# Selection rounds paced by a load table, fp32 products in two parts, and index products two heads behind, in a hybrid recurrence and sparse-attention block

## The chip, the cores and the metric

The kernel runs on one core of one Trainium2 chip. The metric is the device time of one execution in microseconds (us). Its engines are TensorE (PE, matrix products; PEld is its weight load), VectorE (DVE), ScalarE (ACT), GpSimd (POOL) and SyncE (SP), whose queue issues nearly all DMAs. Each engine works through its own instructions in order.

## The reference

One layer over 512 tokens of width 2048. The input is normalised and projected; branch A is a gated linear recurrence (8 heads), branch B attends to 128 keys for each query, which an indexer with 16 heads picks; gates merge the branches, an output projection goes into the residual, and a norm ends it. The parts that matter here:

```
k_idx = layernorm(k_idx_raw)                                  # keys' norm
rel_scores = relu(einsum('bthd,bsd->bths', qi_blk, k_idx))    # index products, 16 heads
score = einsum('bths,bth->bts', rel_scores, wi_blk)
score = where(visible, score, -inf)
top_val, top_idx = top_k(score, 128)                          # selection
bias = bias_table[t5_bucket(top_idx - t_pos)]                 # bias by distance
logits = where(valid, logits + bias, -inf)
# branch A, by chunks: cumulative decays, scores inside a chunk, a state between chunks
```

## The kernel before

**Products.** Every large product is done in high and low float32r parts: `split` (L71) makes the high part on ScalarE and the low part, source minus high part, on VectorE, and `mm3` (L75) does three products of them. Weights come through SP into `wr` (two buffers) and are split into `wh` and `wl` by `prep` (L157), two groups ahead of the products that read them; a load of `wr` is held until VectorE has made the `wl` from that buffer.

**What sets the order.** A hand-written order: a job runs its products on PE and calls `pump` (L189) after every 12 products of 512 columns or 24 of 256. `pump` gives each of six lanes one step, in the order hgrn, top, att, norm, misc, t5. What a lane issues in a step stands in the engines' queues ahead of what comes next. I call the stretch from one pump to the next a step.

**The recurrence** (`hgrn_gen`, L736) runs once for each of four pairs of heads, in the order 3, 2, 0, 1, which I call the first to the fourth recurrence. It has eight levels, a step each. In a level PE computes many small score products `hl` from `hq` and `hk` (L753); then VectorE scales `hq` by decays (L757 in level 0, L764 later) and makes the next decays `tot` (L769), POOL scales `hk` (L766), and a mask copy takes the scores (L780). The next level's `hl` needs `hq` and `hk` scaled. After the levels come state products, and at the end a norm over `hz`, on ScalarE Ln and Exp, then the output block on VectorE (four operations at L841 and L842) and the two parts `hy` of its result.

**The selection** (`top_gen`, L649) finds each query's 128 best keys on VectorE: for three blocks of queries (b = 1, 2, 3, with 256, 384 and 512 columns) 16 rounds each, a round being MAX8 (L663) and MATCH_REPLACE8 (L664), and then a flag pass over the block (L666). How many rounds a step gets is set by a credit: `R.hot` is true in the eight levels, and a step then adds 0.55 rounds; in all others it adds 1.75.

**The index** (`qidx_evac`, L619, and `idx_gen`, L629): a projection tile of a head (12 products of 384 columns) is split into `qih` and `qil`; the head's index products `sc`, nine in three blocks, are put in the lane when the next head's tile has been split, one head behind. ScalarE takes them with a relu and VectorE sums them into `M`.

**Keys' norm** (`kidx_gen`, L596) sums over partitions with a product of ones and plain fp32 data, once for the mean and once for the variance. **The bias** (`t5_gen`, L459) selects bias rows by an fp32 product with a one-hot table (L472), writes them to DRAM (`t5_d`), loads them back shifted by one element a partition (`bf`, two loads of 512 KB), and flips the partitions with an fp32 product (L487) for two heads at a time, four flips.

Of the kernel before, what the change touches and what calls it, by code (L numbers as in the profile page):

```python
# [26 lines left out]
F32 = mybir.dt.float32  # L27
FR = mybir.dt.float32r
AF = mybir.ActivationFunctionType
# [5 lines left out]
T, D = 512, 2048  # L35
NK = D // 128
H, HD = 8, 128
# [13 lines left out]
def hybrid_block(ctx, tc, x, norm_w, w_in, lb_table, gnorm_a, q_norm_w, kv_norm_w, w_uq,  # L51
# [3 lines left out]
    V, A, G, PE, SP = nc.vector, nc.scalar, nc.gpsimd, nc.tensor, nc.sync  # L55
# [38 lines left out]

    ya_d = dram.tile([2, H, 128, T], F32, name="ya_d")
    yb_d = dram.tile([2, H, 128, T], F32, name="yb_d")
    t5_d = dram.tile([H, 384], F32, name="t5_d")
    gate_d = dram.tile([48, 128, T], F32, name="gate_d")
    bh_d = dram.tile([H, 128, 256], F32, name="bh_d")
    m21_d = dram.tile([2, 128, 8, 256], F32, name="m21_d")  # L100
# [12 lines left out]
    def leave(name):  # L113
        pools.pop(name)[0].__exit__(None, None, None)

    R = SimpleNamespace(hot=False)


    specs = []
# [60 lines left out]
    lanes = {name: deque() for name in ("hgrn", "top", "att", "norm", "misc", "t5")}  # L180

    late = [[], []]
# [275 lines left out]

    def t5_gen():  # L459
        rb = R.i.tile([128, H], F32, name="rb")  # L460
        oh = R.i.tile([128, 384], F32, name="oh")
        tl = R.i.tile([H, 384], F32, name="tl")
        flip = R.i.tile([128, 128], F32, name="flip")
        far = R.i.tile([H, 1], F32, name="far")
        G.memset(rb, 0.0)
        SP.dma_start(rb[0:32], rel_bias)
        SP.dma_start(oh, c_buckets)
        SP.dma_start(flip, c_flip)
        yield
        yield  # L470
        ps = bank("t5")
        PE.matmul(ps[:H, :384], rb, oh, start=True, stop=True)  # L472
        V.tensor_copy(far, ps[:H, 0:1])
        V.tensor_scalar(tl, ps[:H, :384], far, None, op0=OP.subtract)
        late[1].append(lambda: SP.dma_start(t5_d, tl))
        yield
        yield
        yield
        for h in range(0, H, 2):
            if h % 4 == 0:  # L480
                bf = R.i.tile([128, 4, 256], F32, name="bf")
                SP.dma_start(bf, bass.AP(tensor=t5_d.tensor, offset=t5_d.offset + h * 384,
                                         ap=[[1, 128], [384, 4], [1, 256]]))
                yield
                yield
            ps = bank("t5")
            PE.matmul(ps, flip, bf[:, h % 4:h % 4 + 2, :], start=True, stop=True)  # L487
            e = R.i.tile([128, 2, 256], F32, name="nt", bufs=2)
            V.tensor_copy(e, ps.rearrange("p (h c) -> p h c", h=2))
            late[1].append(lambda h=h, e=e: SP.dma_start(bh_d[h:h + 2].rearrange("h p c -> p h c"), e))  # L490
            yield
# [102 lines left out]
            yield  # L594

    def kidx_gen():  # L596
        ps = bank("ns")
        mm(ps, ones, R.kx[:, 0, :], True, True)
        t = R.i.tile([128, T], F32, name="nt", bufs=2)
        V.scalar_tensor_tensor(t, ps, -1.0 / 128, R.kx[:, 0, :], op0=OP.mult, op1=OP.add)  # L600
        s = R.i.tile([128, T], F32, name="nsq", bufs=2)
        A.activation(s, t, AF.Square)
        yield
        yield
        ps = bank("ns")
        mm(ps, ones, s, True, True)
# [10 lines left out]
    waiting = []  # L617

    def qidx_evac(h0):  # L619
        def evac(c, ps):  # L620
            qh = R.q.tile([128, 384], FR, name="qih", bufs=2)
            ql = R.q.tile([128, 384], FR, name="qil", bufs=2)
            split(qh, ql, ps)
            if waiting:
                lanes["misc"].append(waiting.pop())
            waiting.append(idx_gen(h0 + c, qh, ql))
        return evac

# [20 lines left out]
    def top_gen():  # L649

        credit = 0.0
        V.memset(R.M[:, 0:128], 0.0)
        for b in range(4):
            V.memset(R.M[0:64, MO[b] + b * 128 + 64:MO[b] + b * 128 + 128], NEG)
        for b in (1, 2, 3):
            m = R.M[:, MO[b]:MO[b] + b * 128 + 128]
            for i in range(16):
                while credit < 1:
                    yield
                    credit += 0.55 if R.hot else 1.75  # L660
                credit -= 1
                m8 = R.s.tile([128, 8], F32, name="m8", bufs=2)
                V.max(m8, m)  # L663
                V.match_replace(m, m8, m, GONE)  # L664
                if i == 15:
                    V.tensor_scalar(m, m, -2e38, NEG, op0=OP.is_gt, op1=OP.mult)  # L666
# [69 lines left out]
    def hgrn_gen(p):  # L736
        f, k, q = (hg[p, n] for n in "fkq")
# [31 lines left out]
            V.tensor_tensor(nt, tv[:, :, 0], tv[:, :, 1], op=OP.mult)  # L769
            return nt  # L770

        R.hot = True
        for l in range(8):
            if l == 4:
                G.memset(S, 0.0)
            ps = bank("hl")
            scores(l, ps)
            tot = decay(l)
            if l < 6:
                V.copy_predicated(near, R.levels[:, l:l + 1, :].to_broadcast([128, 8, 32]),  # L780
                                  ps[:, 0:256].rearrange("p (n t) -> p n t", n=8))
# [10 lines left out]
        R.hot = False  # L792
        kd = R.h.tile([128, 2, 3, 128], F32, name="hkd")
        for c in range(2):
            pt = bank("hkt")
# [3 lines left out]
        yield  # L799
        while (p, "v") not in hg:  # L800
            yield
        v = hg[p, "v"]
        st = R.h.tile([128, 2, 3, 128], F32, name="hst")
        for c in range(2):
# [13 lines left out]
        for c in range(2):  # L818
            po = bank("ho")
            for j in range(4):  # L820
                sl = slice(j * 128, (j + 1) * 128)
                mm(po[:, sl], v[:, j, c * 128:(c + 1) * 128], S[:, 4 * c + j, :], j == 0, j == 0)
                if j:
                    mm(po[:, sl], st[:, c, j - 1, :], q[:, c, sl], False, True)
            A.activation(o[:, c], po, AF.Copy)
            A.activation(sq[:, c], po, AF.Square)
            yield
            zs.append((place(p, [128, T], FR, "hzh", ("hkd", "hst")[c]),
                       place(p, [128, T], FR, "hzl", ("hq", "hS")[c])))
            split(*zs[c], sq[:, c])  # L830
        yield
        for c in range(2):
            ps = bank("hz")
            mm(ps, ones_r, zs[c][0], True, False)
            mm(ps, ones_r, zs[c][1], False, True)
            A.activation(sq[:, c], ps, AF.Ln, bias=eps, scale=1.0 / 128)
        A.activation(sq, sq, AF.Exp, scale=-0.5)
        yield
        for c in range(2):
            r = sq[:, c]  # L840
            V.scalar_tensor_tensor(r, o[:, c], c_gw, r, op0=OP.mult, op1=OP.mult)  # L841
            V.tensor_tensor(r, r, gate[:, c], op=OP.mult)  # L842
        yield
        for c in range(2):
            y = [place(p, [128, T], FR, f"hy{i}", (("hkd", "hst"), ("hq", "hS"))[i][c]) for i in range(2)]
            split(*y, sq[:, c])
            for i in range(2):
                late[1].append(lambda y=y[i], i=i, h=2 * p + c: SP.dma_start(ya_d[i, h], y.bitcast(F32)))
# [308 lines left out]
                 qidx_evac(2 * p), width=384)  # L1157

    def end_index():
        lanes["misc"].append(waiting.pop())  # L1160
# [363 lines left out]
```

## Time and profile before

| what | us |
|---|---|
| runs of the kernel before (three) | 1381.38, 1379.5, 1381.48; median 1381.38 |
| the profiled execution's own time | 1379.72 |
| its span, first to last instruction | 1377.9 |
| PE busy | 1353.1 |
| VectorE busy | 1072.2 |
| ScalarE busy | 654.3 |
| POOL busy | 83.0 |

The profile is one execution. Times in its rows count from the span's start. In a timeline row the first number is the start, the second how long it took; a matmul's record is longer than the time by which it holds back the next one, because products overlap in the array, so what a product costs is read from end to end or from start to start. In brackets stands the engine's idle time before the row and what ended it. The granted clock is TensorE's, as a share of 2.4 GHz; it knows two levels, 2.4 and 1.2 GHz.

### The profile page before, as it was taken

The page shows a single profiled execution, that of the slowest core. Times are in us where ns is not written, and L with a number is a line of the kernel's source. Part 1 is how long each engine was busy: PE and PEld are TensorE (multiplying, and loading weights), DVE is VectorE, ACT ScalarE, POOL GpSimd, SP SyncE. Part 2 cuts the span into 40 slices and gives each one's busy share as a digit, 9 for nine tenths or more (in the row PEclk, how much of TensorE's full clock was granted, in tenths as well). Part 3 has the DMA queues.
Part 4 walks back from the last instruction along what each step waited for, and adds up shares of the span by engine and source line. Part 5 has one row for each costly group of instructions (what it writes and reads, how often), then busy time and mean ns, then how long its engine had stood idle before and what let it go on. Part 6 is the DMA issues. An engine that isn't in the chain of part 4 may idle for free. (4 is left out here: it accounts for less than half of the span.)

```text
span 1377.9 us, 26785 instructions
## 1 busy us (share of the span) xinstructions
PE 1353.1 (98%) x10940; PEld 1253.3 (91%) x10940; DVE 1072.2 (78%) x1738; ACT 654.3 (47%) x1047; POOL 83.0 (6%) x85
## 2 busy tenths in 40 slices
PE   8999999999999999999999989999999999999997
PEld 7888999999999999998989778878888888899996
DVE  7796889988898888877777889675556558899856
ACT  6545445545554444446734442635534333454435
POOL 2100000000000000000030303050101100000000
PEclk9999999999999999999999999999999999999999
DMA  6334345444444344445234323434755556643464
GB/s 205 93 107 138 108 138 169 153 138 143 134 153 136 114 135 138 153 138 188 65 104 121 120 56 120 134 114 141 274 191 192 188 179 218 211 146 121 157 211 168
DMA packets 143597, 203.73 MB, mean 148 GB/s; under 512 B 10433, under 2 KB 84850, under 8 KB 143346
## 3 DMA queue, kind: packets, MB, share of 16 engines
q1 hardware_dynamic: 143186, 201.69, 46.0%
q8 instruction: 86, 1.41, 0.4%
q10 hardware_dynamic: 288, 0.33, 0.1%
q14 instruction: 37, 0.30, 0.1%
HBM read 166.84 MB, written 35.14 MB: 147 GB/s over the span
## 5 line engine op out<-in xcount | busy, mean ns | idle before, releaser
L150 ACT ACTIVATE bh<-wr 128x768 fp32r<-128x768 f32 x128 | 108.1, 845 | 220.5 <-issue 119.6
L152 ACT ACTIVATE wh<-sv 128x512 fp32r<-128x512 f32 x256 | 151.7, 622 | 85.2 <-DVE sv L145 66.2
L73 DVE TENSOR_TENSOR wl<-wr,wh 128x1024 fp32r<-128x1024 f32 (+1 forms) x104 | 127.1, 1222 | 61.0 <-ACT wh L72 60.6
L78 PE MATMUL pp<-sh,wl 128*128 128x256 f32 x624 | 172.8, 277 | 0.0
L76 PE MATMUL pp<-sh,wh 128*128 128x256 f32 x624 | 172.8, 277 | 0.0
L77 PE MATMUL pp<-sl,wh 128*128 128x256 f32 x624 | 172.7, 277 | 0.0
L153 DVE TENSOR_TENSOR bl<-wr,bh 128x768 fp32r<-128x768 f32 x128 | 122.3, 956 | 54.4 <-ACT bh L150 54.0
L72 ACT ACTIVATE wh<-wr 128x1024 fp32r<-128x1024 f32 (+1 forms) x104 | 108.1, 1040 | 116.8 <-PE acc L77 59.7
L154 DVE TENSOR_TENSOR wl<-sv,wh 128x1024 fp32r<-128x1024 f32 x128 | 156.5, 1223 | 7.5 <-ACT wh L152 1.1
L76 PE MATMUL acc<-xh,wh 128*128 128x512 f32 x304 | 122.4, 403 | 0.0
L78 PE MATMUL acc<-xh,wl 128*128 128x512 f32 x304 | 118.7, 391 | 0.0
L77 PE MATMUL acc<-xl,wh 128*128 128x512 f32 x304 | 118.5, 390 | 0.0
L77 PEld LDWEIGHTS pp<-sl,wh 128*128 128x128 f32 x624 | 117.3, 188 | 0.0
L78 PEld LDWEIGHTS pp<-sh,wl 128*128 128x128 f32 x624 | 117.3, 188 | 0.0
L76 PEld LDWEIGHTS pp<-sh,wh 128*128 128x128 f32 x624 | 117.3, 188 | 0.0
L76 PE MATMUL pp<-xh,bh 128*128 128x256 f32 x416 | 114.9, 276 | 0.0
L77 PE MATMUL pp<-xl,bh 128*128 128x256 f32 x416 | 114.9, 276 | 0.0
L78 PE MATMUL pp<-xh,bl 128*128 128x256 f32 x416 | 114.9, 276 | 0.0
L76 PE MATMUL acc<-yh,wh 128*128 128x512 f32 x256 | 100.2, 392 | 0.0
L78 PE MATMUL acc<-yh,wl 128*128 128x512 f32 x256 | 99.8, 390 | 0.0
L77 PE MATMUL acc<-yl,wh 128*128 128x512 f32 x256 | 99.7, 390 | 0.0
L145 DVE TENSOR_TENSOR sv<-wr 128x512 f32<-128x512 f32 x128 | 87.9, 687 | 7.3 <-DMA wr<-in_w_in_dram 3.6
(384 smaller groups left out, 3693.4 us busy)
## 6 DMA issues: line engine op xcount, KB each, us to landing
wr<-in_w_in_dram SPq DMA_DIRECT2D x136, 512.0 KB, 3.6
wr<-in_w_out_dram SPq DMA_DIRECT2D x32, 512.0 KB, 3.7
mg<-gate_d SPq DMA_DIRECT2D x48, 256.0 KB, 3.9
gate_d<-c SPq DMA_DIRECT2D x44, 256.0 KB, 5.0
wr<-in_w_in_dram SPq DMA_DIRECT2D x36, 256.0 KB, 3.1
wr<-in_w_pa_dram SPq DMA_DIRECT2D x16, 512.0 KB, 4.7
wr<-in_w_pb_dram SPq DMA_DIRECT2D x16, 512.0 KB, 3.2
x<-in_x_dram SPq DMA_DIRECT2D x8, 512.0 KB, 6.5
```

The costliest lines, as they stand in the source:

```text
L72: A.activation(hi, src, AF.Copy)
L73: V.tensor_tensor(lo, src, hi.bitcast(F32), op=OP.subtract)
L76: PE.matmul(ps, lh, rh, start=first, stop=False, skip_group_check=True)
L77: PE.matmul(ps, lh, rl, start=False, stop=False, skip_group_check=True)
L78: PE.matmul(ps, ll, rh, start=False, stop=last, skip_group_check=True)
L145: V.tensor_tensor(sv[:, 0:2, :], b[:, 1:3, :], b[:, 0:1, :].to_broadcast([128, 2, 256]), op=OP.add)
L150: A.activation(bh, b[:, 1:4, :], AF.Copy)
L152: A.activation(vh[:, i:i + 2, :], sv[:, i:i + 2, :], AF.Copy)
L153: V.tensor_tensor(bl, b[:, 1:4, :], bh.bitcast(F32), op=OP.subtract)
L154: V.tensor_tensor(vl, sv, vh.bitcast(F32), op=OP.subtract)
```

## The change

Four edits.

1. **Rounds by room.** `R.hot` becomes `R.load`, a number in us that the recurrence sets for every step (eight values for the levels, others for the steps behind them). `top_gen` adds 2.7 less the load to its credit each step, and a round takes 0.4 + 0.27 (b + 1) from it: 0.94, 1.21 and 1.48 for the three blocks. A round is put out as long as the credit is above zero. All 48 rounds end in the same step as before.
2. **Keys' norm in two parts.** Each of the two sums splits its source and does two float32r products in place of one in fp32; the split takes a step of its own.
3. **The bias in two parts.** Table, bias rows and flip matrix become float32r; the bias rows are split and written to DRAM in both parts, loaded back in eight loads of 256 KB (two for each pair of heads), and each flip is two float32r products. The table's product lies one step later, and the flips are spread over steps three apart. On SP's queue the first two of the `bf` loads now stand behind the weight load that was behind the first `bf` load before; each later pair also stands behind a weight load.
4. **Index products two heads behind.** Three buffers of `qih` and `qil` in place of two; a head's products go into the lane when two more tiles have been split. The last three heads are drained together.

```diff
-    t5_d = dram.tile([H, 384], F32, name="t5_d")
+    t5_d = dram.tile([2, H, 384], F32, name="t5_d")
...
-    R = SimpleNamespace(hot=False)
+    R = SimpleNamespace(load=0.0)
...
         ps = bank("t5")
-        PE.matmul(ps[:H, :384], rb, oh, start=True, stop=True)
+        for i, r in enumerate(rbs):
+            mm(ps[:H, :384], r, oh, i == 0, i == 1)
         V.tensor_copy(far, ps[:H, 0:1])
         V.tensor_scalar(tl, ps[:H, :384], far, None, op0=OP.subtract)
-        late[1].append(lambda: SP.dma_start(t5_d, tl))
+        split(*ts, tl)
+        for i in range(2):
+            late[1].append(lambda i=i: SP.dma_start(t5_d[i], ts[i].bitcast(F32)))
...
+            bf = R.i.tile([128, 2, 2, 256], FR, name="bf")
...
-            PE.matmul(ps, flip, bf[:, h % 4:h % 4 + 2, :], start=True, stop=True)
+            for i in range(2):
+                mm(ps, flip, bf[:, i].rearrange("p h c -> p (h c)"), i == 0, i == 1)
...
     def kidx_gen():
-        ps = bank("ns")
-        mm(ps, ones, R.kx[:, 0, :], True, True)
+        def spread(src):
+            sh = R.i.tile([128, T], FR, name="sumh")
+            sl = R.i.tile([128, T], FR, name="suml")
+            split(sh, sl, src)
+            yield
+            ps = bank("ns")
+            mm(ps, ones_r, sh, True, False)
+            mm(ps, ones_r, sl, False, True)
+            return ps
+
+        ps = yield from spread(R.kx[:, 0, :])
...
-            if waiting:
-                lanes["misc"].append(waiting.pop())
+            if len(waiting) > 1:
+                lanes["misc"].append(waiting.pop(0))
...
-                while credit < 1:
+                while credit <= 0:
                     yield
-                    credit += 0.55 if R.hot else 1.75
-                credit -= 1
+                    credit += 2.7 - R.load
+                credit -= 0.4 + 0.27 * (b + 1)
...
-        R.hot = True
         for l in range(8):
+            R.load = (1.7, 2.5, 2.1, 1.8, 1.8, 1.7, 1.3, 1.3)[l]
...
+        R.load = 2.9
         for c in range(2):
             r = sq[:, c]
             V.scalar_tensor_tensor(r, o[:, c], c_gw, r, op0=OP.mult, op1=OP.mult)
```

What this moves is seen in the engines' orders. VectorE ahead of the third recurrence, before: the last row (L842) of the output block of the recurrence before, then rounds (MAX and MATCH_REPLACE on `M`), the flag pass (L666) and the low parts `hy`. Behind these rows come `wl`, one more round and level 0's `hq`.

```order
L842 TENSOR_TENSOR hk<-hk,hg 128x512
L663 MAX m_9796<-M 128x8
L664 MATCH_REPLACE M<-m_9796,M 128x384
L663 MAX m_9799<-M 128x8
L664 MATCH_REPLACE M<-m_9799,M 128x384
L666 TENSOR_SCALAR M<-M 128x384
L73 TENSOR_TENSOR hy_9828<-hk,hy_9827 128x512
L73 TENSOR_TENSOR hy_9832<-hk,hy_9831 128x512
L663 MAX m_9835<-M 128x8
L664 MATCH_REPLACE M<-m_9835,M 128x512
L663 MAX m_9838<-M 128x8
L664 MATCH_REPLACE M<-m_9838,M 128x512
```

The same place on VectorE now, from the output block's last row to the mask copy behind level 0's `hq` (L774 is the former L757).

```order
L864 TENSOR_TENSOR hk<-hk,hg 128x512
L73 TENSOR_TENSOR hy_9869<-hk,hy_9868 128x512
L73 TENSOR_TENSOR hy_9873<-hk,hy_9872 128x512
L680 MAX m_9876<-M 128x8
L681 MATCH_REPLACE M<-m_9876,M 128x512
L73 TENSOR_TENSOR wl<-wr,wh 128x1024
L680 MAX m_9914<-M 128x8
L681 MATCH_REPLACE M<-m_9914,M 128x512
L774 TENSOR_TENSOR hq<-hq,hf 128x1024
L797 COPY_PREDICATED hnear<-levels,hl 128x256
```

Between the output block and `hq` stood five rounds and a flag pass; there are two rounds now. The others stand in earlier steps.

VectorE ahead of the second recurrence, before, from the low parts `hy` of the first recurrence's output to level 0's `hq`; two more rounds stand ahead of these rows, behind the output block.

```order
L73 TENSOR_TENSOR hy_9120<-hk,hy_9119 128x512
L73 TENSOR_TENSOR hy_9124<-hk,hy_9123 128x512
L663 MAX m_9127<-M 128x8
L664 MATCH_REPLACE M<-m_9127,M 128x256
L663 MAX m_9130<-M 128x8
L664 MATCH_REPLACE M<-m_9130,M 128x256
L663 MAX m_9150<-M 128x8
L664 MATCH_REPLACE M<-m_9150,M 128x256
L73 TENSOR_TENSOR wl<-wr,wh 128x1024
L757 TENSOR_TENSOR hq<-hq,hf 128x1024
```

The same place now, from the `wl` that follows the output block; `nt` (L499) is the copy of a flipped bias.

```order
L73 TENSOR_TENSOR wl<-wr,wh 128x1024
L73 TENSOR_TENSOR hy_9158<-hk,hy_9157 128x512
L73 TENSOR_TENSOR hy_9162<-hk,hy_9161 128x512
L680 MAX m_9165<-M 128x8
L681 MATCH_REPLACE M<-m_9165,M 128x256
L683 TENSOR_SCALAR M<-M 128x256
L680 MAX m_9186<-M 128x8
L681 MATCH_REPLACE M<-m_9186,M 128x384
L499 COPY nt<-t_9189 128x512
L73 TENSOR_TENSOR wl<-wr,wh 128x1024
L774 TENSOR_TENSOR hq<-hq,hf 128x1024
```

The block of 256 columns is now at its last round here and its flag pass stands ahead of `hq` instead of behind it; a bias copy has come in, and there are two rounds where five stood.

VectorE at the start of the index, before: `qil` are the low parts of the heads' tiles (two heads in one row), and L643 takes the first head's index products into `M`.

```order
L73 TENSOR_TENSOR wl<-wr,wh 128x1024
L73 TENSOR_TENSOR qil<-acc,qih 128x384 x2
L643 TENSOR_SCALAR M<-relu,widx 128x512
L643 TENSOR_SCALAR M<-relu,widx 128x384
L643 TENSOR_SCALAR M<-relu,widx 128x256
L73 TENSOR_TENSOR wl<-wr,wh 128x1024
L73 TENSOR_TENSOR qil<-acc,qih 128x384
```

The same place now (L660 is the former L643).

```order
L73 TENSOR_TENSOR wl<-wr,wh 128x1024
L73 TENSOR_TENSOR qil<-acc,qih 128x384 x2
L73 TENSOR_TENSOR wl<-wr,wh 128x1024
L73 TENSOR_TENSOR qil<-acc,qih 128x384
L660 TENSOR_SCALAR M<-relu,widx 128x512
L660 TENSOR_SCALAR M<-relu,widx 128x384
L660 TENSOR_SCALAR M<-relu,widx 128x256
```

The third head's low part has moved ahead of the first head's sums, as on PE the third head's projection has moved ahead of the first head's index products.

## Rows read from the trace of the kernel before

**Rows 1.** The page's first part: busy time of each engine, its share of the span, instructions.

```profile
PE 1353.1 (98%) x10940; PEld 1253.3 (91%) x10940; DVE 1072.2 (78%) x1738; ACT 654.3 (47%) x1047; POOL 83.0 (6%) x85
```

**Rows 2.** Who PE waited for, by line: us in total, times, longest.

```profile
PE hl L81 <- DVE hq L757: 6.2, 2, 5.3
...
PE sc L76 <- ACT qih L72: 1.2, 1, 1.2
PE hl L81 <- POOL hk L766: 1.1, 1, 1.1
PE hl L81 <- DVE tot L769: 1.0, 1, 1.0
PE sc L78 <- DVE qil L73: 0.6, 1, 0.6
```

**Rows 3.** Busy time by stretch: stretch and its length; busy us and instructions of PE, PEld, DVE, ACT, POOL; granted clock; DMA share; GB/s.

```profile
700.00:720.00 20.00, 18.92 (x358) 17.49 (x357) 14.69 (x21) 9.84 (x17) 7.92 (x7) 1.00 0.27 82
...
820.00:830.00 10.00, 4.69 (x87) 4.43 (x87) 9.83 (x17) 0.00 (x0) 1.50 (x1) 0.69 0.46 130
830.00:840.00 10.00, 10.00 (x256) 9.49 (x255) 9.93 (x17) 2.28 (x4) 3.88 (x3) 0.97 0.57 190
```

**Rows 4.** PE's timeline in the third recurrence, levels 0 to 1.

```profile
820.97 0.28 PE L77 MATMUL acc<-wl,xh 128*128 128x256 f32 x1
821.08 0.28 PE L78 MATMUL acc<-wh,xl 128*128 128x256 f32 x1
826.66 1.08 PE L81 MATMUL hl<-hq,hk 128*32 128x32 f32 x64 [5.31 <-DVE hq L757]
...
828.06 0.42 PE L77 MATMUL acc<-wl,xh 128*128 128x256 f32 x1
828.27 0.41 PE L78 MATMUL acc<-wh,xl 128*128 128x256 f32 x1
```

**Rows 5.** VectorE's timeline ahead of that.

```profile
812.06 1.23 DVE L73 TENSOR_TENSOR wl<-wr,wh 128x1024 fp32r<-128x1024 f32 x1 [2.46 <-ACT wh L72]
813.20 0.75 DVE L841 SCALAR_TENSOR_TENSOR hk<-ho,cols,hk 128x512 f32<-128x512 f32 x1
...
815.98 0.56 DVE L663 MAX8 m<-M 128x8 f32<-128x384 f32 x1
...
818.76 1.29 DVE L73 TENSOR_TENSOR hy<-hk,hy 128x512 fp32r<-128x512 f32 x2
819.96 0.69 DVE L663 MAX8 m<-M 128x8 f32<-128x512 f32 x1
...
821.47 0.69 DVE L663 MAX8 m<-M 128x8 f32<-128x512 f32 x1
...
822.87 1.22 DVE L73 TENSOR_TENSOR wl<-wr,wh 128x1024 fp32r<-128x1024 f32 x1
...
825.39 1.22 DVE L757 TENSOR_TENSOR hq<-hq,hf 128x1024 f32<-128x1024 f32 x1
```

**Rows 6.** VectorE's and PE's timelines at the start of the second recurrence.

```profile
751.40 0.42 DVE L663 MAX8 m<-M 128x8 f32<-128x256 f32 x1
...
758.41 1.22 DVE L73 TENSOR_TENSOR wl<-wr,wh 128x1024 fp32r<-128x1024 f32 x1
759.54 1.22 DVE L757 TENSOR_TENSOR hq<-hq,hf 128x1024 f32<-128x1024 f32 x1
...
760.81 0.76 PE L81 MATMUL hl<-hq,hk 128*32 128x32 f32 x64 [0.85 <-DVE hq L757]
```

**Rows 7.** PE's and VectorE's timelines at the first index products.

```profile
628.74 0.50 PE L76 MATMUL sc<-kih,qih 128*128 128x512 f32 x1 [1.24 <-ACT qih L72]
...
631.33 0.33 PE L76 MATMUL acc<-cqh,wh 128*128 128x384 f32 x1
...
633.41 0.40 PE L76 MATMUL sc<-kih,qih 128*128 128x512 f32 x1
...
635.00 0.33 PE L76 MATMUL acc<-cqh,wh 128*128 128x384 f32 x1
...
629.49 1.01 DVE L73 TENSOR_TENSOR qil<-acc,qih 128x384 fp32r<-128x384 f32 x2
```

**Rows 8.** PE's timeline at the first sum of keys' norm (one fp32 product has two records).

```profile
60.48 0.40 PE L78 MATMUL acc<-xh,wl 128*128 128x512 f32 x1
60.72 1.02 PE L81 MATMUL ns<-kx,ones_r 128*128 128x512 f32 x2
61.17 0.80 PE L76 MATMUL acc<-xh,wh 128*128 128x512 f32 x1
```

**Rows 9.** VectorE's timeline behind that: the block that prepares the paired inputs, and the next low part.

```profile
66.32 1.22 DVE L1027 TENSOR_TENSOR sv<-xh,xl 128x1024 f32<-128x1024 f32 x1
...
69.04 1.22 DVE L73 TENSOR_TENSOR wl<-wr,wh 128x1024 fp32r<-128x1024 f32 x1
```

**Rows 10.** SP's timeline in the first recurrence (a weight load that was held), and a row of the DMA view: issues, KB each, median us from issue to landing.

```profile
712.11 9.25 SPq L128 DMA_DIRECT2D wr<-in_w_in_dram  x2
...
hg<-gate_d SPq DMA_DIRECT2D x4, 512.0 KB, 5.1
```

**Rows 11.** VectorE's and POOL's timelines in the second recurrence, level 2.

```profile
765.91 1.81 DVE L764 TENSOR_TENSOR hq<-hq,tot 128x512 f32<-128x512 f32 x1
...
765.36 1.81 POOL L766 TENSOR_TENSOR hk<-hk,tot 128x512 f32<-128x512 f32 x1 [2.18 <-PE hl L81]
```

More of the change, by code (lines that the diff above doesn't have):

```diff
@@ L460, in t5_gen @@
         rb = R.i.tile([128, H], F32, name="rb")
-        oh = R.i.tile([128, 384], F32, name="oh")
+        rbs = [R.i.tile([128, H], FR, name=f"rb{i}") for i in "hl"]
+        oh = R.i.tile([128, 384], FR, name="oh")
         tl = R.i.tile([H, 384], F32, name="tl")
-        flip = R.i.tile([128, 128], F32, name="flip")
+        ts = [R.i.tile([H, 384], FR, name=f"tl{i}", tag=f"sum{i}") for i in "hl"]
+        flip = R.i.tile([128, 128], FR, name="flip")
         far = R.i.tile([H, 1], F32, name="far")
@@ L466, in t5_gen @@
         SP.dma_start(rb[0:32], rel_bias)
-        SP.dma_start(oh, c_buckets)
-        SP.dma_start(flip, c_flip)
+        raw = R.i.tile([128, 512], F32, name="nt", bufs=2)
+        SP.dma_start(raw[:, 0:384], c_buckets)
+        SP.dma_start(raw[:, 384:], c_flip)
         yield
         yield
+        A.activation(oh, raw[:, 0:384], AF.Copy)
+        A.activation(flip, raw[:, 384:], AF.Copy)
+        split(*rbs, rb)
+        yield
         ps = bank("t5")
-        PE.matmul(ps[:H, :384], rb, oh, start=True, stop=True)
+        for i, r in enumerate(rbs):
+            mm(ps[:H, :384], r, oh, i == 0, i == 1)
         V.tensor_copy(far, ps[:H, 0:1])
         V.tensor_scalar(tl, ps[:H, :384], far, None, op0=OP.subtract)
-        late[1].append(lambda: SP.dma_start(t5_d, tl))
-        yield
-        yield
-        yield
-        for h in range(0, H, 2):
[L480 to L485, printed above, removed]
+        split(*ts, tl)
+        for i in range(2):
+            late[1].append(lambda i=i: SP.dma_start(t5_d[i], ts[i].bitcast(F32)))
+        for _ in range(3):
+            yield
+        for h in range(0, H, 2):
+            bf = R.i.tile([128, 2, 2, 256], FR, name="bf")
+            for i in range(2):
+                SP.dma_start(bf[:, i].bitcast(F32), bass.AP(tensor=t5_d.tensor, offset=t5_d.offset + (i * H + h) * 384,
+                                                            ap=[[1, 128], [384, 2], [1, 256]]))
+            yield
+            yield
             ps = bank("t5")
-            PE.matmul(ps, flip, bf[:, h % 4:h % 4 + 2, :], start=True, stop=True)
+            for i in range(2):
+                mm(ps, flip, bf[:, i].rearrange("p h c -> p (h c)"), i == 0, i == 1)
             e = R.i.tile([128, 2, 256], F32, name="nt", bufs=2)
@@ L596, in kidx_gen @@
     def kidx_gen():
-        ps = bank("ns")
-        mm(ps, ones, R.kx[:, 0, :], True, True)
+        def spread(src):
+            sh = R.i.tile([128, T], FR, name="sumh")
+            sl = R.i.tile([128, T], FR, name="suml")
+            split(sh, sl, src)
+            yield
+            ps = bank("ns")
[3 more added lines that the diff above has]
+        ps = yield from spread(R.kx[:, 0, :])
         t = R.i.tile([128, T], F32, name="nt", bufs=2)
@@ L603, in kidx_gen @@
         yield
-        yield
-        ps = bank("ns")
-        mm(ps, ones, s, True, True)
+        ps = yield from spread(s)
         r = rstd_row(ps, 128)
@@ L620, in evac @@
         def evac(c, ps):
-            qh = R.q.tile([128, 384], FR, name="qih", bufs=2)
-            ql = R.q.tile([128, 384], FR, name="qil", bufs=2)
+            qh = R.q.tile([128, 384], FR, name="qih", bufs=3)
+            ql = R.q.tile([128, 384], FR, name="qil", bufs=3)
             split(qh, ql, ps)
-            if waiting:
-                lanes["misc"].append(waiting.pop())
+            if len(waiting) > 1:
+                lanes["misc"].append(waiting.pop(0))
             waiting.append(idx_gen(h0 + c, qh, ql))
@@ L790, in hgrn_gen @@
             yield
-        R.hot = False
+        R.load = 0.0
         kd = R.h.tile([128, 2, 3, 128], F32, name="hkd")
@@ L801, in hgrn_gen @@
             yield
+        R.load = 1.4
         v = hg[p, "v"]
@@ L826, in hgrn_gen @@
             A.activation(sq[:, c], po, AF.Square)
+            R.load = 0.7 * c
             yield
@@ L830, in hgrn_gen @@
             split(*zs[c], sq[:, c])
+        R.load = 0.7
         yield
+        R.load = 0.0
         for c in range(2):
@@ L843, in hgrn_gen @@
         yield
+        R.load = 1.3
         for c in range(2):
@@ L1159, in end_index @@
     def end_index():
-        lanes["misc"].append(waiting.pop())
+        lanes["misc"].extend(waiting)
         drain("misc")
```

## The prediction

> **What bounds the kernel now.** The page's first part comes first: PE is busy 98% of the span and every other engine at most 78% [rows 1]. The end is therefore set by PE's own work and by the places where PE stands still, and an edit is worth what it takes out of one or the other. The second view is PE's waits: those that are left are few, and five of them lie in the code that the diff touches [rows 2]. The largest single one is 5.3 us, PE's score products hl waiting for VectorE's product hq (L757). The third view, busy time and granted clock by stretches, says where it is and that it costs more than its length: in 820 to 830 us PE is busy 4.69 of 10 us and the granted clock is 0.69, in 830 to 840 still 0.97, while 700 to 720, where PE also stood for about 1 us, has 1.00 [rows 3]. 0.69 and 0.97 are a mean of the two levels 2.4 and 1.2 GHz: (1 - 0.69) x 10 / 0.5 = 6.2 us at the low level before 830, and 0.6 us after it.
>
> **The rounds, third recurrence (pair 0): the largest term.** PE's timeline has its last product ending at 821.36 (821.08 + 0.28), then nothing until 826.66. Behind the gap a 256-column product takes 0.21 us of PE (828.06 to 828.27) where it took 0.11 (820.97 to 821.08) [rows 4]: the low level. From 826.66 to 830.6 that is 3.9 us of which half, 1.9 us, is lost. So this place costs 5.3 + 1.9 = 7.2 us.
> VectorE's timeline says why hq is late [rows 5]. From 813.20 it runs the output block of the recurrence before (L841, L842) until 815.98, two rounds of 384 columns and their flag pass until 818.76, the low parts hy until 819.96, two rounds of 512 until 822.87, a weight's low part wl, one more round, and hq from 825.39 to 826.61. The order of the changed kernel has on the same stretch: block, both hy, one round of 512, wl, one round, hq. From the same start at 815.98, with 1.2 us for hy and 0.1 for the ScalarE copy ahead of its second half (an estimate), 1.51 for a round (819.96 to 821.47), 1.13 for wl, 1.51, and 1.22 for hq, hq ends at 822.7. PE would start at 822.75 instead of 826.66: 3.9 us are gone and a wait of 1.4 us stays. That is near the 1.0 us that left the clock at 1.00 and far from 5.3, so I take the low clock away as well: 1.9 us. What is late next is the step behind it: after hq come a mask copy (0.4, an estimate), a round (1.51), wl (1.13) and the next hq (0.7, an estimate), 3.7 us and with a start at 822.7 ready at 826.4 to 826.7, while PE arrives 3.55 us after its start, at 826.3: a new wait of up to 0.4. Sum 3.9 + 1.9 - 0.4 = **5.4 us**. Bounds: 7.2 if nothing waits, 2.3 if 3 us of wait stay and the clock still falls.
>
> **The rounds, second recurrence (pair 2).** There PE waits 0.85 us at 760.81 for an hq that VectorE begins only at 759.54. The output block ended at 751.40 and five rounds of 256 columns stand between, the last work ahead of hq being wl at 758.41 [rows 6]. In the new order 15 of the 16 rounds of 256 come before the block instead of 10. Behind the block stand wl (1.1), two hy (1.2), one round of 256 and its flag pass (1.4, an estimate), one round of 384 (1.25, half of 815.98 to 818.76 without the flag pass), a bias copy nt (0.7, an estimate), wl (1.1) and hq (1.2): 8.0 us. Before, PE came to need hq at 760.81 - 0.85 = 759.96, 8.6 us after the block's end, and it now has two pairs of flips more in that stretch (0.9): 9.5 us. The wait goes, with 1.5 us to spare: **0.9 us**, bounds 0 and 0.9. In the steps behind it the table asks for a round in six of eight steps where five stood; each step has a period of 3.6 us and the nearest margin I find is 0.6 us. The fourth recurrence has no rounds before or after (all 48 are out by the same weight step), so its wait of 1.1 us for POOL [rows 2] stays.
>
> **Index products two heads behind.** The first product waits 1.24 us for the high part qih. Then the three products of that head take 2.59 us (628.74 to 631.33) where the next head's take 1.59 (633.41 to 635.00): 1.0 us more, for the low part qil, which VectorE makes from 629.49 to 630.5 for two heads [rows 7]. Now twelve products of the next projection (631.33 to 633.41, 2.08 us) come first, so that the first index product starts at about 627.5 + 2.08 = 629.6 and needs the low part 0.45 later, at 630.05, when its half of VectorE's 1.01 us is just done. **2.2 us**, bounds 1.7 and 2.3. At the far end three heads instead of two are drained in a row; PE does the same products, and ScalarE and VectorE see the same work behind them, so I cost that at nothing; if PE had to wait for a bank there, it would cost up to the 1.6 us of one head's products.
>
> **High and low parts for keys' norm and bias.** One fp32 product over 512 columns occupies PE from the end before it (60.48 + 0.40 = 60.88) to its own end (60.72 + 1.02 = 61.74), 0.86 us; the float32r product behind it adds 0.23 (to 61.17 + 0.80 = 61.97) [rows 8]. Two float32r products in place of one fp32 save 0.40. There are six of them (two for the norm, four flips), 2.4 us, and the table's product with three quarters of the columns, 0.3. Against it: the second sum of the norm now needs a low part which VectorE makes behind a block of five operations (66.32 to 69.04, 2.72 us) and a wl [rows 9]; laid after PE's two steps that is about 0.3 us late, bounds 0 and 1.2. The table's 0.3 is mostly not kept: in the first recurrence PE waits 1.0 us for VectorE anyway (the stretch 700 to 720) [rows 2, 3], and that chain now carries the table's high and low part as well; I keep 0.1. Sum 2.4 - 0.3 + 0.1 = **2.2 us**, bounds 1.2 and 2.7.
> The bias loads become eight of 256 KB where two of 512 KB were, and on SP's queue the first pair now stands behind a weight load that is held until VectorE has freed its buffer (712.11) instead of ahead of it. A 512 KB load issued behind a weight load landed after 5.1 us [rows 10]; 712.9 + 5 = 718 is just ahead of the flip, at some 718.5. Later pairs have more room. Cost nothing, up to 1 us if it lands behind.
>
> **A rule that speaks against it.** hq took 1.81 us when POOL's hk ran beside it, from 765.36 to 767.17 [rows 11], against the 0.7 used above; with fewer rounds ahead of it, hq will more often start together with hk. By the row that adds 1.1 us to the step behind the long wait: its 0.4 becomes 1.5, and the total of all terms 9.6. The Trainium skill (SBUF — State Buffer, "Who interferes with whom") says that a VectorE instruction with two SBUF inputs and a GpSimd instruction that reads SBUF exclude each other, the later one waiting out the other's whole length; the row of 1.81 agrees with it.
>
> **Rivals.** (A) The wait in the third recurrence goes altogether and the first recurrence's 1.0 goes with it: 7.2 + 0.9 + 2.2 + 2.7 + 1.0 = 14.0 us. For it: five rounds and a flag pass fall to two rounds between the output block and hq. Against: from 815.98 the sum above leaves no way to 821.4. (B) hq meets hk on POOL at the tight step, as above: 9.6 us. For it: rounds that kept the two apart are gone. Against: there hk starts first and VectorE still has a round and wl to do. (C) ScalarE's chain ahead of the output block, not the rounds, keeps VectorE late: 3 us of the long wait stay and the low clock with them, 2.3 + 0.5 + 2.2 + 1.7 = 6.7 us. For it: VectorE's wl at 812.06, which the block stands behind, had itself waited for ScalarE. (D) The change makes it slower: the bias loads land late at each of the four flips. From 4 us of lateness each PE stands 16 us in all and falls to the low clock four times (4 x 1.9), against 10.7 of gains: 13 us slower. It needs landings of 9 us where 5.1 is the nearest row, so I give it little. (E) The table does not do what it is for: hq is as late as before in both recurrences, or a step elsewhere pays for it, and only the products' saving stays, about 2.5 us, within the 0.2%.
>
> **How the numbers follow.** Gain 5.4 + 0.9 + 2.2 + 2.2 = 10.7 us. The profiled execution took 1379.72 us, of which 1377.9 are span; from it 1369.0. It lies at the fast end of the runs (1379.5 to 1381.48, median 1381.38), from the median it is 1370.7; I put the forecast between, **1369.8 us**. Chances: forecast 0.47; A 0.18 (1365.7 to 1367.4); B 0.14 (1370.1 to 1371.8); C 0.12 (1373 to 1374.7); D 0.04 (1382 to 1394.5); E 0.05 (1377 to 1379). The range reaches over A, B and C: 1365.5 to 1374.5. Faster by over 0.2% (2.8 us, about what a measurement of this kernel can tell from no change): the forecast, A, B and C, 0.91; within it E, 0.05; slower D, 0.04.
>
> **What would show it.** In PE's waits the 5.3 for hq should be at most 1.6, with the granted clock at 1.00 in all stretches between start and tail; the wait of the second recurrence and both waits of sc should be gone, those of tot (1.0) and hk (1.1) still there. PE's busy time should be about 4.5 us less (2.5 from the products, 1.9 from the clock). I am wrong about the rounds if hq is still 3 us late with rounds ahead of it, wrong about the precision edit if PE waits for suml or for bf, and wrong about the products if two float32r passes take more than 0.5 us.

## The result, and the profile after

| what | before | after |
|---|---|---|
| runs, median | 1381.1 (four runs, 1379.5 to 1381.48) | 1372.36 (four runs, 1372.0 to 1372.79) |
| profiled execution and its span | 1379.72, 1377.9 | 1372.18, 1370.3 |
| PE busy | 1353.1 | 1348.0 |

The ratio is 0.9939, with a 95% interval of 0.9922 to 0.9956: 8.7 us by the medians, 6.1 to 10.8 by the interval. The forecast was 1369.8, the measured time lies 2.6 us above it and inside the range.

The first 40 us of an execution vary by up to 1.1 us, whatever the kernel (how soon `x` lands, and whether the clock is at its low level for a while: from 10 to 20 us it is 1.00 in the profile before and 0.83 in the one after). So I also measure a kernel between two PE instructions that every kernel here has: an early product that waits for `widx`, and the `hl` of the fourth recurrence that waits for POOL's `hk`. From the second one to the end every kernel here takes 462.3 to 462.6 us. PE's timeline of the kernel before, then of the one after:

```profile
37.64 0.46 PE L339 MATMUL acc<-diag,ones_r 128*128 128x128 f32 x2 [0.27 <-DVE widx L385]
...
915.64 0.76 PE L81 MATMUL hl<-hq,hk 128*32 128x32 f32 x64 [1.14 <-POOL hk L766]
```

```profile
38.01 0.46 PE L339 MATMUL acc<-diag,ones_r 128*128 128x128 f32 x2 [0.27 <-DVE widx L385]
...
907.97 0.76 PE L81 MATMUL hl<-hq,hk 128*32 128x32 f32 x64 [1.14 <-POOL hk L783]
```

The distance is 878.00 us before and 869.96 after: 8.04 us shorter. I call this the stretch below.

Who PE waited for, after, answers to [rows 2]: line, us in total, times, longest.

```profile
PE sc L76 <- ACT relu L655: 2.4, 2, 1.6
...
PE hl L81 <- DVE hq L774: 1.2, 1, 1.2
PE hl L81 <- POOL hk L783: 1.1, 1, 1.1
PE hl L81 <- DVE tot L786: 1.0, 1, 1.0
...
PE hl L81 <- DVE hq L781: 0.6, 2, 0.4
```

The 5.3 of level 0's `hq` has become 1.2, the second recurrence's 0.85 is gone, `qih` and `qil` are gone; `tot` and `hk` are still there. The first row is new: 2.4 us of the index products waiting for ScalarE's relu. Busy time and granted clock by stretches, as in [rows 3]:

```profile
820.00:830.00 10.00, 9.47 (x252) 9.04 (x253) 9.97 (x15) 1.06 (x1) 4.46 (x3) 1.00 0.72 243
830.00:840.00 10.00, 10.00 (x201) 8.13 (x200) 9.24 (x16) 2.49 (x4) 4.37 (x5) 1.00 0.37 107
```

The stretch that had 4.69 us of PE and a clock of 0.69 now has 9.47 and 1.00. VectorE's timeline there, which answers to [rows 5]:

```profile
813.54 1.48 DVE L73 TENSOR_TENSOR hy<-hk,hy 128x512 fp32r<-128x512 f32 x2
814.93 0.69 DVE L680 MAX8 m<-M 128x8 f32<-128x512 f32 x1
...
817.46 0.69 DVE L680 MAX8 m<-M 128x8 f32<-128x512 f32 x1
...
818.85 1.22 DVE L774 TENSOR_TENSOR hq<-hq,hf 128x1024 f32<-128x1024 f32 x1
...
821.71 1.86 DVE L73 TENSOR_TENSOR wl<-wr,wh 128x1024 fp32r<-128x1024 f32 x1
823.49 0.68 DVE L781 TENSOR_TENSOR hq<-hq,hf 128x512 f32<-128x512 f32 x1
```

Between the two parts `hy` and `hq` stand two rounds, 1.4 us each from start to the start of what follows, and a `wl`. POOL's row beside the second `wl`:

```profile
820.97 1.51 POOL L783 TENSOR_TENSOR hk<-hk,hf 128x512 f32<-128x512 f32 x1 [37.87 <-PE hl L81]
```

PE's timeline answers to [rows 4]: the last product before each wait, and the `hl` behind it.

```profile
818.63 0.28 PE L78 MATMUL acc<-wh,xl 128*128 128x256 f32 x1
820.12 0.76 PE L81 MATMUL hl<-hq,hk 128*32 128x32 f32 x64 [1.21 <-DVE hq L774]
...
823.63 0.28 PE L78 MATMUL acc<-wh,xl 128*128 128x256 f32 x1
824.32 0.75 PE L81 MATMUL hl<-hq,hk 128*32 128x32 f32 x64 [0.41 <-DVE hq L781]
```

The bias's two products, on PE (answers to [rows 8], where one fp32 product held PE for 0.86):

```profile
731.35 0.39 PE L81 MATMUL ho<-hq,hst 128*128 128x128 f32 x2
731.49 0.71 PE L81 MATMUL t<-bf,flip 128*128 128x512 f32 x2
```

From 731.74 to 732.20, 0.46 for both.

**The new wait.** PE's timeline at the second and third group of index products, after:

```profile
637.08 0.40 PE L78 MATMUL sc<-kih,qil 128*128 128x512 f32 x1
638.20 0.45 PE L76 MATMUL sc<-kih,qih 128*128 128x384 f32 x1 [0.72 <-ACT relu L655]
...
641.73 0.40 PE L78 MATMUL sc<-kih,qil 128*128 128x512 f32 x1
643.78 0.44 PE L76 MATMUL sc<-kih,qih 128*128 128x384 f32 x1 [1.65 <-ACT relu L655]
```

Each time the first block of a head (512 columns) runs and the second stands: the bank it wants is given back by the relu of the head before. ScalarE's timeline, after:

```profile
630.23 1.26 ACT L655 ACTIVATE relu<-sc 128x512 f32<-128x512 f32 x3 [0.26 <-PE sc L78]
...
636.18 0.81 ACT L728 ACTIVATE hf<-hf,lb,oml 128x512 f32<-128x512 f32 x1 [2.55 <-DMA hf<-qf_d]
...
637.57 1.23 ACT L655 ACTIVATE relu<-sc 128x512 f32<-128x512 f32 x3
640.44 1.06 ACT L72 ACTIVATE wh<-wr 128x1024 fp32r<-128x1024 f32 x1 [1.64 <-DMA wr<-in_w_qidx_dram]
...
643.15 1.23 ACT L655 ACTIVATE relu<-sc 128x512 f32<-128x512 f32 x3
```

and the same place before:

```profile
634.30 1.30 ACT L638 ACTIVATE relu<-sc 128x512 f32<-128x512 f32 x3 [0.20 <-PE sc L78]
...
637.66 0.81 ACT L711 ACTIVATE hf<-hf,lb,oml 128x512 f32<-128x512 f32 x1
...
640.96 1.06 ACT L72 ACTIVATE wh<-wr 128x1024 fp32r<-128x1024 f32 x1 [0.68 <-DMA wr<-in_w_qidx_dram]
```

Before, a head's relu stood ahead of `hf` (a copy that prepares the recurrence's input, `forget`), and `hf`'s load had landed by then. Now each head's relu stands one step later, so `hf` and a weight's high part `wh` stand ahead of it, and ScalarE stands there for both loads. The weight load comes hardly earlier than before, 640.44 against 640.96. SP's timeline and the DMAs by stretch (the last three numbers are the clock, the DMA share and GB/s) say why:

```profile
629.85 0.47 SPq L456 DMA_DIRECT2D hf<-qf_d  x1
...
631.54 11.62 SPq L128 DMA_DIRECT2D wr<-in_w_qidx_dram  x3
```

```profile
630.00:640.00 10.00, 9.28 (x54) 8.66 (x53) 4.84 (x10) 4.33 (x9) 0.72 (x1) 1.00 1.04 342
```

The DMA engines are full at 342 GB/s from 630 to 640, and the weight load stands in the queue behind four loads of 512 KB, `hq` and `hf` of two pairs.

### The profile page after: what moved, and what is told of

Its sections match the earlier page's. It is cut to its first block, busy times and chain, and to the rows that moved or that the text cites. A ratio compares the mean times of both kernels' runs of the same rounds, so it can differ in the third digit from the quotient of the medians.

```text
span 1370.3 us, 26813 instructions
## 1 busy us (share of the span) xinstructions
PE 1348.0 (98%) x10940; PEld 1250.9 (91%) x10940; DVE 1072.1 (78%) x1742; ACT 656.6 (48%) x1053; POOL 82.8 (6%) x85
```

## The experiments

"Stretch" is the distance defined above, of the one profiled execution; the ratio is to the kernel before, run on the same chip. The medians, each taken against the kernel before on its own chip, give the same signs, but differ from the stretch by up to 0.7 us, so a difference of some tenths rests on the rows shown with it and not on the stretch alone.

| run | median us | ratio, 95% interval | stretch us | against |
|---|---|---|---|---|
| before | 1381.1 | | 878.00 | |
| after | 1372.36 | 0.9939 (0.9922 to 0.9956) | 869.96 | before -8.04 |
| index alone | 1381.66 | 1.0009 (1.0 to 1.0018) | 879.52 | before +1.52 |
| rounds alone | 1374.08 | 0.9956 (0.9942 to 0.997) | 872.16 | before -5.84 |
| parts alone | 1376.85 | 0.9977 (0.9968 to 0.9985) | 874.88 | before -3.12 |
| hf a step later | 1374.62 | 0.9964 (0.9951 to 0.9976) | 872.60 | after +2.64 |
| index one behind | 1371.14 | 0.9931 (0.9918 to 0.9943) | 868.86 | after -1.10 |
| loads later | 1369.67 | 0.9923 (0.991 to 0.9937) | 868.16 | after -1.80 |
| no rounds ahead | 1369.49 | 0.992 (0.9907 to 0.9934) | 867.78 | after -2.18 |
| both | 1368.44 | 0.9913 (0.9899 to 0.9926) | 866.50 | after -3.46 |
| all three | 1367.10 | 0.9901 (0.9886 to 0.9916) | 865.64 | after -4.32 |
| three rounds | 1373.77 | 0.9948 (0.9934 to 0.9963) | 872.78 | after +2.82 |
| four rounds | 1376.13 | 0.9969 (0.9956 to 0.9981) | 874.80 | after +4.84 |

### One edit at a time

**Index alone**, in the kernel before:

```diff
-            qh = R.q.tile([128, 384], FR, name="qih", bufs=2)
+            qh = R.q.tile([128, 384], FR, name="qih", bufs=3)
...
-            if waiting:
-                lanes["misc"].append(waiting.pop())
+            if len(waiting) > 1:
+                lanes["misc"].append(waiting.pop(0))
```

> Only the index products two heads behind are put into the kernel before. Theory T (the relu of a head now stands on ScalarE behind a copy hf that is held for its load, and PE runs out of score banks): PE no longer waits 2.4 us at the first index products but 2.9 us at the second and third group, so 0.5 us slower than before, within what can be told from no change. Rival A (the prediction's term stands, something else in the changed kernel ate it): 2.2 us faster.

Measured 1.5 us more in the stretch, and 1381.66 against 1380.17 for the kernel before on the same chip, with an interval that begins at 1.0. The waits for `qih` and `qil` are gone and 2.3 us of waits for the relu are there. The edit loses by itself; nothing else in the changed kernel took its gain. Of the 1.5 us, 1.0 is the edit's own: from the early product to the first recurrence's first `hl` are 652.23 us before and 653.18 here. The other 0.5 stands in the third recurrence, which the edit does not touch. The long wait for `hq` is the same there (5.3 us), but more of the time at the low clock lies behind it. Busy time in the 10 us behind that wait (the third number from the end is the granted clock): before, index alone, and parts alone, which comes below.

```profile
826.66:836.66 10.00, 10.00 (x242) 9.60 (x243) 9.93 (x16) 1.06 (x1) 2.94 (x3) 0.80 0.72 238
828.05:838.05 10.00, 10.00 (x234) 9.64 (x237) 9.93 (x15) 1.06 (x1) 3.28 (x2) 0.74 0.71 235
823.65:833.65 10.00, 10.00 (x245) 9.60 (x246) 9.93 (x16) 1.06 (x1) 3.19 (x3) 0.82 0.70 237
```

That is 4.0, 5.2 and 3.6 us of work at the low level, of which half is lost.

**Rounds alone**: `top_gen` and the `R.load` lines of the changed kernel in the kernel before.

```diff
-                while credit < 1:
+                while credit <= 0:
                     yield
-                    credit += 0.55 if R.hot else 1.75
-                credit -= 1
+                    credit += 2.7 - R.load
+                credit -= 0.4 + 0.27 * (b + 1)
```

> Only the selection rounds by the load table are put into the kernel before. Theory T (the terms add up): 5.3 + 0.9 = 6.2 us faster, the granted clock 1.00 in 820 to 840 us, one wait of some 1.2 us and one of some 0.4 left in the third recurrence. Rival B (part of the gain there is owed to the flips and the norm being shorter, so that VectorE and PE meet differently): 4.5 us faster or less, or a new wait of 1 us or more in the first or second recurrence.

Measured: 5.84 us in the stretch, 6.1 by the medians. PE's waits for `hq` are 1.2 and 0.5 us, that of the second recurrence is gone. Theory T holds; the gain needs neither of the other edits.

**Parts alone**: `t5_gen` and `kidx_gen` of the changed kernel in the kernel before.

```diff
-        mm(ps, ones, R.kx[:, 0, :], True, True)
+        ps = yield from spread(R.kx[:, 0, :])
...
-            PE.matmul(ps, flip, bf[:, h % 4:h % 4 + 2, :], start=True, stop=True)
+            for i in range(2):
+                mm(ps, flip, bf[:, i].rearrange("p h c -> p (h c)"), i == 0, i == 1)
```

> Only the high and low parts for the keys' norm and the bias are put into the kernel before. Theory T: 0.5 (norm) + 0.4 (table) + 1.7 (four flips) = 2.6 us faster. Rival C (with five rounds still ahead of hq, VectorE's extra splits and bias copies fall on the late hq of the second recurrence): 0.85 us of wait there grows to 1.5 or more, so at most 2.0 us faster.

Measured: 3.12 us in the stretch, 3.3 by the medians. The waits for `hq` total 6.0 instead of 6.2, so rival C falls. Two things in the 3.12 are not the edit's: the wait for `qih` is 0.36 us shorter in this execution (0.88 against 1.24), and the third recurrence gains 0.2 because less of the low clock lies behind its wait (the rows above). Without them it is 2.5, near theory T's 2.6.

The three edits alone sum to 5.84 + 3.12 - 1.52 = 7.44 us of the 8.04. About 0.3 of the missing 0.6 is that shift of the low clock, which costs 0.5 in index alone and gives 0.2 in parts alone, while the changed kernel has no low clock there; I can't place the rest.

### What makes the index wait

**`hf` a step later**, in the changed kernel, so that one head's relu stands ahead of `hf` again:

```diff
-            for _ in range(3):
+            for _ in range(4 if p == 3 else 3):
                 yield
             forget(p, 0)
```

> The changed kernel with the first pair's copies hf and hk one step later on ScalarE, behind the relu that stands behind them now. Theory T: the wait of 0.7 us at the second group of index products goes, and that of 1.65 us at the third falls to 1.3 us or less, since there ScalarE still stands for a weight load; 1.0 to 2.4 us faster than the changed kernel, 9.7 to 11 us faster than before. Rival D (the loads that land late set the pace, whatever stands in front of the relu): within 0.5 us of the changed kernel.

Both were wrong: 2.64 us slower. PE's waits and ScalarE's timeline of this run, then its stretch behind 640 us:

```profile
PE sc L76 <- ACT relu L655: 3.5, 1, 3.5
```

```profile
641.25 1.06 ACT L72 ACTIVATE wh<-wr 128x1024 fp32r<-128x1024 f32 x1 [6.17 <-DMA wr<-in_w_qidx_dram]
```

```profile
640.00:650.00 10.00, 6.51 (x28) 5.89 (x27) 6.39 (x10) 8.28 (x16) 0.00 (x0) 0.83 0.24 80
```

The first wait is gone, and PE runs on until it meets the weight load all at once: 3.5 us instead of 0.7 and 1.65, and this single wait takes the clock down to 0.83 of the stretch. (1 - 0.83) x 10 / 0.5 is 3.4 us at the low level, half of which, 1.7, is lost; with 1.1 us more waiting that is 2.8, near the 2.64. So the order on ScalarE is not the cause by itself: the landing of the weight load is the point that PE can't pass, and the two short waits were the cheaper way to reach it.

**Index one behind**: edit 4 undone in the changed kernel (two buffers, `if waiting`, as before).

> The changed kernel with the index products one head behind again, as before. Theory L (the weight load that lands at 640.4 to 641.3 us, behind 2 MB of hq and hf loads, holds ScalarE and so the index; what PE gains ahead of that landing it loses at it): the waits of 0.7 and 1.65 us (2.9 with what lies around them) go and the 2.4 at the first product come back, so 0.5 us faster than the changed kernel. The prediction's term: 2.2 us slower.

Measured 1.10 us less in the stretch (0.5 by the medians): the relu waits are gone, `qih` (0.9) and `qil` (0.6) are back. Up to the first recurrence's first `hl` the distance is 651.42 us against 652.41 in the changed kernel. Put in alone the edit cost 1.0 up to there, and taken out it gives 1.0, so with the loads where they stood it costs 1.0 us.

**Loads later**, in the changed kernel: the four loads leave `open_branches` and are issued by `early_gen`, each pair at its own steps.

```diff
-            for i, n in enumerate("qf"):
-                SP.dma_start(hg[p, n], qf_d[i, 2 * p - 4:2 * p - 2].rearrange("f p t -> p f t"))
...
         for p in (3, 2):
+            for i, n in ((1, "f"), (0, "q")):
+                SP.dma_start(hg[p, n], qf_d[i, 2 * p - 4:2 * p - 2].rearrange("f p t -> p f t"))
             for _ in range(3):
                 yield
```

> The changed kernel with the loads of hf and hq a step (first pair) and six steps (second pair) later on SP's queue, behind a weight load for the index instead of ahead of it, hf ahead of hq. Theory L: the weight load lands at 633 to 635 instead of 640.4, both new waits of the index go, 2.0 to 2.9 us faster than the changed kernel. Theory T (ScalarE's order, not the loads, makes the wait): 0.7 us faster at most.

Measured 1.80 us less in the stretch. ScalarE's timeline and PE's wait of this run:

```profile
635.07 0.82 ACT L726 ACTIVATE hf<-hf,lb,oml 128x512 f32<-128x512 f32 x1 [2.51 <-DMA hf<-qf_d]
...
637.57 1.07 ACT L72 ACTIVATE wh<-wr 128x1024 fp32r<-128x1024 f32 x1
```

```profile
PE sc L76 <- ACT relu L653: 0.7, 1, 0.7
```

`wh` no longer waits for its load: the 1.65 are gone. `hf` still waits for its own, which lands at 635, and the 0.7 stay. The load theory holds for the larger wait, ScalarE's order for the smaller one; the expected 2.0 to 2.9 took both for one.

### How much the rounds ahead of hq are worth

**No rounds ahead**, in the changed kernel:

```diff
-        R.load = 2.9
+        R.load = 4.4 if p == 2 else 2.9
...
-        R.load = 1.3
+        R.load = 2.7 if p == 2 else 1.3
```

> The changed kernel with a larger load for the steps behind the second recurrence's output block, so that no round stands between that block and hq of the third recurrence, and none in its first level; they come later. If rounds are what makes hq late, the waits of 1.2 and 0.4 us in the third recurrence (2.0 with what lies around them) go: 1.5 to 2.0 us faster than the changed kernel. Rival C of the prediction (ScalarE's chain ahead of the output block): a wait of 0.8 us or more stays, 0.5 us faster at most. Third case: the moved rounds meet the end of the selection and cost it back.

Measured 2.18 us less in the stretch. VectorE's timeline of this run, from the `wl` ahead of the output block, and PE's `hl`:

```profile
808.49 1.23 DVE L73 TENSOR_TENSOR wl<-wr,wh 128x1024 fp32r<-128x1024 f32 x1 [1.54 <-ACT wh L72]
...
812.40 1.47 DVE L73 TENSOR_TENSOR hy<-hk,hy 128x512 fp32r<-128x512 f32 x2
814.13 1.23 DVE L73 TENSOR_TENSOR wl<-wr,wh 128x1024 fp32r<-128x1024 f32 x1 [0.25 <-ACT wh L72]
815.27 1.22 DVE L774 TENSOR_TENSOR hq<-hq,hf 128x1024 f32<-128x1024 f32 x1
...
817.71 0.76 PE L81 MATMUL hl<-hq,hk 128*32 128x32 f32 x64
```

`hq` is ready at 816.49, 1.2 us before the `hl` that needs it, which starts at 817.71 without a wait; one wait of 0.2 us for `hq` is left in the whole kernel. ScalarE's chain (rival C) holds VectorE for 1.54 us ahead of the output block and 0.25 behind it, and `hq` is early even so: the rounds made it late. The rounds that moved bring no new wait of PE. Of the 2.18, 0.35 is not the edit's: the first wait of the index products is 0.37 us in this execution and 0.72 in the changed kernel's. That leaves 1.8, inside the expected 1.5 to 2.0.

**Three and four rounds**, in the changed kernel: 1.4 and 0.0 in place of 4.4 in the diff above, without its second change.

> The changed kernel with one round of 512 columns more between the second recurrence's output block and hq of the third recurrence (three instead of two). If each round there moves hq by its own 1.5 us, PE's wait is 2.7 us instead of 1.2. With the clock at 1.00 that costs 1.5 us against the changed kernel; if the clock falls, as the prediction's lower bound took it for a wait of 3 us, 3 to 3.4 us.

> The changed kernel with two rounds more there (four instead of two). PE's wait is 4.2 us; with the clock at 1.00 that costs 3.0 us against the changed kernel, with the clock fallen for the 3.4 us that the run with hf alone showed behind its wait of 3.5 us, 4.7 us, for 6.8 us as in the kernel before, 6.4 us.

PE's wait and the stretch with three rounds:

```profile
PE hl L81 <- DVE hq L774: 2.4, 1, 2.4
```

```profile
820.00:830.00 10.00, 9.31 (x232) 8.95 (x234) 9.10 (x13) 1.06 (x1) 3.28 (x2) 0.83 0.76 255
```

and with four:

```profile
PE hl L81 <- DVE hq L774: 3.9, 1, 3.9
```

```profile
820.00:830.00 10.00, 7.82 (x161) 7.59 (x162) 8.41 (x14) 1.06 (x1) 2.37 (x2) 0.66 0.84 264
```

The waits are 0, 1.2, 2.4, 3.9 and, before, 5.3 us with 0, 2, 3, 4 and 5 rounds (and a flag pass) ahead. The clock is 1.00 with the first two, then 0.83 (3.4 us at the low level), 0.66 (6.8 us) and 0.69 and 0.97 (6.8 us). With three rounds the stretch is 2.82 us longer: 1.2 of wait, 0.4 less at the next level, 1.7 of clock, which leaves 0.3 for two waits of 0.2 elsewhere. With four it is 4.84: 2.7 of wait less 0.4, which leaves 2.5 for the clock. Of the 6.8 us at the low level part lies in the wait itself: in the 10 us behind the wait the clock is 0.72, 5.6 us at the low level. The expectations for these clocks, 3.0 to 3.4 and 6.4, were 0.2 and 1.6 too high: both waits came out 0.3 shorter, 0.4 came back at the next level, and the four-round one counted the whole low stretch as work.

### Put together

**Both** is the later loads and no rounds ahead in one kernel.

> The changed kernel with both edits, the later loads and no rounds ahead of the third recurrence. If the two are independent, the sum: 3.5 to 4.9 us faster than the changed kernel, 11.5 to 13 us faster than before.

Measured 3.46 us less in the stretch, against 1.80 + 2.18 = 3.98 for the two alone, and just under the expected 3.5 to 4.9. Most of the gap is the 0.35 named above, which is a wait of the index and so counted in both. **All three** adds the later `hf`, which lost 2.64 us when the loads were where they had been:

```diff
-            for _ in range(3):
+            for _ in range(4 if p == 3 else 3):
```

> The kernel of the run before (later loads, no rounds ahead of the third recurrence) and the first pair's copies hf and hk one step later on ScalarE. There the second group of index products still waits 0.6 us (0.85 with what lies around it) for a relu behind hf, whose load lands at 635. Theory L with ScalarE's order as its second half: with the weight load landed early, the later hf takes this wait away too, 0.8 us faster than that kernel, 4.5 to 5 us faster than the changed kernel. Rival: as with the hf moved alone, the wait turns up one step later, no gain or a loss of 1 us.

Measured 0.86 us less than both. ScalarE's timeline of this run:

```profile
633.52 1.30 ACT L653 ACTIVATE relu<-sc 128x512 f32<-128x512 f32 x3 [0.21 <-PE sc L78]
634.71 1.06 ACT L72 ACTIVATE wh<-wr 128x1024 fp32r<-128x1024 f32 x1
```

The relu follows its products, `wh` finds its load landed, and no index product waits. Up to the first recurrence's first `hl` this kernel needs 649.65 us, index one behind 651.42. The two waits left there with one head behind (0.9 and 0.6) are for `qih` and `qil` and not for a load, so I take most of the 1.8 us for the index edit's gain, which shows once the loads' order has changed. That is argued, not shown: no run has the later loads with the index one head behind. At 1367.10 us, 13.3 below the kernel before on the same chip, it beats both kernels.

## Why the prediction was right, and where not

The sum was 5.4 + 0.9 + 2.2 + 2.2 = 10.7 us; 8.7 came by the medians, 8.04 in the stretch.

- **Rounds (5.4 + 0.9): right.** 5.84 alone in the stretch, 6.1 by the medians. The wait that was to stay is 1.21 (1.4 foretold, with 1.51 us for a round, which took 1.4), that of the next step 0.41 (up to 0.4), the clock is at 1.00, the second recurrence's wait is gone. Runs with zero to four rounds show the cause: with none `hq` is early, and a third and a fourth round ahead of it move PE by 1.2 and 1.5 us. The lower bound (3 us of wait still lower the clock) was right too, though a wait of 2.4 does it already.
- **Index (2.2): wrong in sign, the step that failed.** The prediction said that ScalarE and VectorE "see the same work behind them" and looked for a cost only where the last heads are drained. What it left out is that a relu one step later stands behind what ScalarE does in that step, `hf` and `wh`, and that PE, 4 us ahead in its projections by then (the fifth tile starts at 634.53 instead of 638.67), meets two loads that no edit had moved. So 2.2 us of gain became 1.0 of loss. The first product's wait did go, as worked out. The rows were there before the change: 640.96 with its wait for the load, and four loads ahead of it on SP's queue (issued from 629.84 on, the weight load at 632.37).
- **Parts (2.2): right in kind, too small.** 3.12 alone, some 2.5 of it the edit's own. A pair of products saves 0.39 (0.85 to 0.46), as worked out; `suml` is late by 0.28 us once, where 0.3 stood; no product waits for `bf`. The table's saving was kept, which I had counted at 0.1: from end to end its pair takes 0.35 where the fp32 product took 0.78. The rest of the 0.9 is the shorter wait for `qih` and the shift of the low clock, and neither is owed to the edit.
- **POOL beside VectorE (rival B).** The price was real, the place another: not `hq` but the `wl` ahead of it took 1.86 us beside POOL's `hk`, where 1.22 is its length. In the kernel before, the same `wl` took 2.19 (at 828.25) beside the same `hk`, so the price was no new one. With it the next step's wait came to the 0.4 foretold, not 1.5. The Trainium skill's rule (SBUF — State Buffer, "Who interferes with whom") is about a VectorE instruction with two SBUF inputs, which `wl` has too. The trace agrees: `hk` ends at 822.48, 0.77 us behind the start of `wl`, and `wl` is 0.64 longer.
- **Rivals A, C, D, E fall.** 1.0 for `tot` is still there and 1.2 of `hq` stays (A), ScalarE's chain holds VectorE ahead of the block with no rounds too, and `hq` is early then (C), no flip waits (D), both `hq` waits moved (E).

So the total held in part by luck. The index term was 3.2 us too good; a parts term up to 0.9 too small made up some of it; and the 2.0 that the sum still was too large by (by the medians) fitted into a range drawn wide for other rivals, none of which had this cause.

## What to carry to other kernels

When one engine is let run ahead, read what every queue behind it has in that step, loads above all: a gain ahead of a load that is held by full DMA engines is given back at its landing, and the order of the loads has to change first. A filler on an engine that feeds the bound costs its own length at most as long as the wait leaves the clock alone; where the wait lowers the clock it costs more (here one round more, about 1.5 us, cost 2.8, and two, about 3, cost 4.8). Of two ways to the same landing, several short waits were cheaper here than one long one.

## What the runs showed of the hardware that I had not expected

A single PE wait of 2.41 us was enough for the granted clock to be at the low level for 3.4 us behind it, while two waits of 0.72 and 1.65 us, with 3.9 us of work between them, left it at 1.00. Waits of 3.5 and 3.9 us gave 3.4 and 6.8 us at the low level: the time lost to the clock does not grow evenly with the wait.
